# Expert weights in runs of 4 KB, three of four down blocks as fp32r passes, 128-column stationary operands

## The chip, the cores and the metric

The kernel runs on one core of one Trainium2 chip. The metric is the device time of one launch in microseconds. Three runs of the kernel before took 1442.43 to 1444.31 us, with a median of 1444.3 us. One further execution was profiled; all rows below are from it.

## The reference

One encoder layer on 1024 tokens of width 1024, in float32: a modulated RMSNorm, a combined input projection, latent attention and differential attention, an output projection, and a mixture of experts. Only the last part is touched by the change:

```python
# top-1 group of 4, then top-2 of 8 experts in it; 32 experts in all
g = xb @ w_gate[e]                     # xb: the rows routed to expert e, 1024 wide
u = xb @ w_up[e]                       # w_gate, w_up: 1024 x 512
ys = (jax.nn.silu(g) * u) @ w_down[e]  # w_down: 512 x 1024
out = out.at[row_token].add(ys * row_weight)
```

After it the residual is added and a last RMSNorm is applied. Each expert has 6 MB of weights, 201 MB for all 32.

## The kernel before

Everything ahead of the experts (projections, both attentions, output projection, router) takes the first 790 us or so and is left as it is, but for the weight loads that already start there. Then the 32 experts follow one another in a loop that is unrolled in Python (L1386). Each works on C = 96 rows, which a gather on POOL fetches from h2_d by index. The instructions stand in the order in which the code writes them; nothing reorders them, and each engine takes its own in that order.

**Precision.** A float32 product on TensorE is done in one of two ways. The first is a plain f32 matmul, which the profile shows as two instructions. The second is `mm3` (L66 to L69): both operands are split into a high part, rounded to fp32r, and a low part, the rest; three fp32r matmuls (high by high, high by low, low by high) add up in PSUM. A weight is split by `split_e` (L1149 to L1154): ScalarE casts 128x1024 values to the high part (L1152), VectorE subtracts to get the low part (L1153). Gate and up use `mm3`; down uses plain f32.

**Weights.** `load_w` (L1129) loads six pieces of 1 MB per expert: four of gate and up, with four row blocks of 128 x 512 each, in runs of 2 KB (a partition p holds rows p, 128 + p, 256 + p, 384 + p), and two of down, each all four row blocks of one half of the columns, again in runs of 2 KB. They go into 14 buffers. `load_free` (L1139) marks a piece as used and starts the next load: at first 14 pieces ahead, from the queue of SP; from piece 84 on the distance shrinks step by step to 7, and then the loads are issued from ScalarE's queue, between its computing instructions.

**Splits.** `split_to` (L1159) issues splits ahead of their use: a gate or up chunk (two of the eight row blocks, one split) asks for splits up to five chunks ahead (three from expert 28 on). The split parts live in a ring of 14 buffers (`ring_a`), two per split; one of the 14 holds `gate2` throughout, so at most six splits are alive.

**One expert e on TensorE:** 24 fp32r passes of gate (four chunks); 4 transposes of the hidden rows of expert e - 1 (`hidden_T`, L1338); 24 passes of up; down of expert e - 1 for the first 512 columns (`down`, L1344); 8 transposes of the rows of expert e + 1 (`x_T`, L1364); down for the other 512 columns; then POOL scatters the result, with accumulation, into x2_d. VectorE scales the down result per column half (L1351). After expert 20, `further_blocks` (L1287) is computed once on VectorE and POOL. The last expert's rows are not scattered but added by a matmul with a selection matrix (L1443), while x2_d is read back for the last norm; that read waits for the scatter of expert 30.

The stationary operand of all these matmuls is 128 x 96: one column for each of the 96 rows.

Of the kernel before, what the change touches and what calls it, by code (L numbers as in the profile page):

```python
# [46 lines left out]


@with_exitstack
def tile_hymba(  # L50
# [689 lines left out]
    wu = w_expert_up[0].rearrange("e (k p) f -> e p k f", p=128)  # L740
# [581 lines left out]
    def flip4(src, b):  # L1322
        ptr = ps4.tile([128, 512], F32, name="ptr4", tag="tr")[:, 0:4 * C]
        for i in range(4):
            j = 4 * b + i
            T.transpose(ptr[:, i * C:(i + 1) * C], src[:, j * 128:(j + 1) * 128], ident[:C, :C])  # L1326
        return ptr

    def glu_gate(pg):
        sg = mp.tile([C, DE], F32, name="sg", tag="sg", bufs=1)  # L1330
# [4 lines left out]
        V.tensor_mul(sg, sg, pu)  # L1335
        return sg

    def hidden_T(hm):  # L1338
        ptr = flip4(hm, 0)
        hT = mp.tile([128, 4, C], F32, name="hmT", tag="hmT")  # L1340
        V.tensor_copy(hT.rearrange("p a b -> p (a b)"), ptr)
        return hT

    def down(hT, w, y, n, wcol):  # L1344
        e, w = (w, raws["d", w, n]) if isinstance(w, int) else (None, w)

        pd = ps4.tile([128, 512], F32, name="pd", tag="pd")[:C]
        for k in range(4):
            T.matmul(pd, hT[:, k], w[:, k], start=k == 0, stop=k == 3)  # L1349
        ns = slice(n * 512, n * 512 + 512)  # L1350
        V.scalar_tensor_tensor(y[:, ns], pd, wcol, gate2[:, ns], op0=ALU.mult, op1=ALU.mult)  # L1351
        load_free(("d", e, n))

    def y_tile():
        return mp.tile([C, D], F32, name="y4", tag="y4")

    def half_ps(name, rows=C):
        return ps4.tile([128, DE], F32, name=name, tag=name)[:rows]
# [3 lines left out]
            gather(xbufs[e % NX], tg[:, e:e + 1])  # L1362

    def x_T(xb):  # L1364
        xT = mp.tile([128, 2, 8, C], F32R, name="xT", tag="xT")
        for b in range(2):
            ptr = flip4(xb, b)
            o = [xT[:, l, 4 * b:4 * b + 4].rearrange("p a b -> p (a b)") for l in range(2)]
            A.copy(o[0], ptr)  # L1369
            V.tensor_sub(o[1], ptr, f32(o[0]))  # L1370
        return xT

    def chunk(ps, xT, e, ch):
        split_to(8 * e + ch + 1 + (LEAD if e < ES else LEAD1))
        hi, lo = splits[8 * e + ch]
# [8 lines left out]
    x_in(NX)  # L1384
    prev = None
    for e in range(NE):  # L1386
        pg, pu = half_ps("pg"), half_ps("pu")
        for ch in range(4):
            chunk(pg, xT, e, ch)
        if prev:  # L1390
            hT, y = hidden_T(prev), y_tile()
        sg = glu_gate(pg)
        if e == 0:
            row(5 * D, gate2)
        for ch in range(4, 8):
            chunk(pu, xT, e, ch)
        hm = glu_up(sg, pu)
        if prev:
            down(hT, e - 1, y, 0, wt[:, e - 1:e])
            if e == NE - 1:  # L1400
                hT_last = hidden_T(hm)
# [26 lines left out]
    y = y_tile()  # L1428
    for n in range(2):
        down(hT_last, NE - 1, y, n, wt[:, NE - 1:])  # L1430
    yl = [mp.tile([C, D], F32R, name="yl", tag="xT") for _ in range(2)]
# [42 lines left out]
    with tc.For_i(0, nb, 1) as i:  # L1474
        er = Y.value_load(eii[0:1, 0, bass.ds(i, 1)], min_val=0, max_val=NE - 1)
        cr = mp.tile([128, NBM + 2], F32, name="cr", tag="cr")
        V.scalar_tensor_tensor(cr[:, 0:NBM], io, blk, ei[:, 1], op0=ALU.is_equal, op1=ALU.mult)
        V.reduce_sum(cr[:, NBM:NBM + 1], cr[:, 0:NBM], axis=AX.X)
        V.tensor_scalar(blk, blk, 1.0, None, op0=ALU.add)
        ats, tws = tile_a(F32)[:, 0:C], tile_a(F32)[:, 0:2 * NT].rearrange("p (t k) -> p t k", k=2)  # L1480
        ptw = ps4.tile([128, 512], F32, name="ptw", tag="tr")[:C]
        V.tensor_scalar(ats, iot_s, float(NE), cr[:, NBM:NBM + 1], op0=ALU.mult, op1=ALU.add)
        for j in range(2 * NT):
            t, k = divmod(j, 2)
            oa, tw = (mp.tile([128, w], F32, name=n, tag=n) for w, n in ((C, "oa"), (2, "tw")))
# [18 lines left out]
        hT = hidden_T(glu_up(glu_gate(pgu[0]), pgu[1]))
        y = y_tile()
        for n in range(2):
            down(hT, raw_w(wd[bass.ds(er, 1), :, :, n * 512:(n + 1) * 512].rearrange("a p k f -> (a p) k f")), y, n,
                 cr[:C, NBM + 1:NBM + 2])
# [45 lines left out]
```

## Time and profile before

| | |
|---|---|
| median of three runs | 1444.3 us |
| the profiled execution: own time, span | 1447.06 us, 1445.3 us |
| TensorE busy | 1337.1 us (93% of the span) |
| TensorE weight loads | 961.9 us (67%), beside the matmuls |
| VectorE busy | 993.9 us (69%) |
| ScalarE busy | 681.8 us (47%) |
| POOL busy | 416.9 us (29%) |
| DMA | 361.22 MB, 250 GB/s on average |
| mean granted TensorE clock | 0.962 |

The span is the time from the first to the last instruction; the profiled execution's own time is 1.8 us longer. Shares are averages over stages that have different limits, so the stretch of the experts, from about 790 to 1410 us, is to be read by itself.

### The profile page before, as it was taken

What the parts mean: (1) busy time and instruction counts of PE and PEld (TensorE: products, weight loads), DVE (VectorE), ACT (ScalarE), POOL (GpSimd) and SP (SyncE); (2) the same over time, 40 slices, a digit from 0 to 9 for tenths busy, and PEclk for the clock granted to TensorE, in tenths of its full rate; (3) what the DMA queues carried; (4) which work ended last, traced back from release to release, by engine and by line L of the source; (5) the groups of instructions that cost most, each with busy time, mean ns of one, the idle gap of its engine ahead of it and who ended that gap; (6) DMA issues with size and microseconds to landing.
All of it is one profiled execution on the core that took longest, in us unless ns stands there. A gap on an engine that the chain in (4) does not pass through costs nothing. (4 is left out here: it accounts for less than half of the span.)

```text
span 1445.3 us, 17733 instructions
## 1 busy us (share of the span) xinstructions
PE 1337.1 (93%) x6211; PEld 961.9 (67%) x6211; DVE 993.9 (69%) x1530; ACT 681.8 (47%) x1058; POOL 416.9 (29%) x285
## 2 busy tenths in 40 slices
PE   5799896998999999989995999999999998999993
PEld 4578676986788888878884655566565555656541
DVE  6888553475788888884568766676766668666646
ACT  4642212454766666661214554444554444544523
POOL 3100000002766666650002233333333322111231
PEclk9899898999999999999995999999999999999995
DMA  9537799268043433337968999999988998999956
GB/s 328 150 100 249 198 298 209 55 223 302 1 152 125 139 130 140 132 112 261 340 224 297 339 354 315 348 366 354 345 297 297 327 348 308 347 359 338 372 181 238
DMA packets 197502, 361.22 MB, mean 250 GB/s; under 512 B 20101, under 2 KB 62146, under 8 KB 195874
## 3 DMA queue, kind: packets, MB, share of 16 engines
q1 hardware_dynamic: 132946, 228.97, 47.2%
q10 hardware_dynamic: 57024, 113.25, 21.9%
q0 software_dynamic: 7440, 17.84, 5.2%
q8 instruction: 50, 0.82, 0.2%
q14 instruction: 42, 0.34, 0.1%
HBM read 306.52 MB, written 61.88 MB: 255 GB/s over the span
## 5 line engine op out<-in xcount | busy, mean ns | idle before, releaser
L1153 DVE TENSOR_TENSOR ra<-rb,ra 128x1024 fp32r<-128x1024 f32 x180 | 210.8, 1217 | 42.4 <-ACT ra L1152 42.2
L1152 ACT CAST ra<-rb 128x1024 fp32r<-128x1024 f32 x180 | 181.5, 1050 | 93.4 <-PE pg L69 34.2
L1319 POOL DMA_INDIRECT x_d<-y,tg x32 | 139.2, 4351 | 132.5 <-DVE y L1351 130.3
L1349 PE MATMUL pd<-rb,hmT 128*96 128x512 f32 x368 | 165.1, 592 | 0.0
L604 PE MATMUL s<-ra 128*128 128x512 f32 x448 | 129.5, 405 | 2.5 <-ACT e L625 2.4
L1351 DVE SCALAR_TENSOR_TENSOR y<-pd,wt,ra 96x512 f32<-96x512 f32 x64 | 47.8, 747 | 121.5 <-PE pd L1349 121.5
L67 PE MATMUL pz<-whi,hThi 128*128 128x512 f32 (+2 forms) x320 | 122.3, 382 | 9.6 <-ACT hThi L255 5.1
L625 ACT ACTIVATE e<-s,mx 128x1024 f32<-128x1024 f32 x96 | 107.6, 1120 | 38.5 <-DVE mx L620 21.8
L620 DVE TENSOR_REDUCE mx<-s 128x1 f32<-128x1024 f32 x96 | 116.6, 1217 | 12.2 <-PE s L604 12.2
L68 PE MATMUL pz<-wlo,hThi 128*128 128x512 f32 (+2 forms) x320 | 120.6, 377 | 1.5 <-DVE wlo L131 1.5
L930 POOL DMA_INDIRECT xb<-h_d,tg x31 | 31.5, 1017 | 313.4 <-PE ptr L1326 312.8
L69 PE MATMUL pz<-whi,hTlo 128*128 128x512 f32 (+2 forms) x320 | 116.0, 370 | 0.3 <-DVE hTlo L257 0.3
L67 PE MATMUL pg<-ra,xT 128*96 128x512 f32 x256 | 114.1, 446 | 0.2 <-ACT xT L1369 0.2
L1349 PEld LDWEIGHTS pd<-rb,hmT 128*96 128x96 f32 x368 | 58.2, 163 | 77.6 <-issue 74.5
L68 PE MATMUL pu<-ra,xT 128*96 128x512 f32 x256 | 102.6, 401 | 3.7 <-DVE ra L1153 3.7
L69 PE MATMUL pg<-ra,xT 128*96 128x512 f32 x256 | 102.1, 399 | 2.8 <-DVE xT L1370 2.8
L67 PE MATMUL pu<-ra,xT 128*96 128x512 f32 x256 | 103.7, 405 | 0.0
L1153 DVE TENSOR_TENSOR ra<-rx,ra 128x1024 fp32r<-128x1024 f32 x76 | 89.6, 1217 | 19.2 <-ACT ra L1152 19.2
L636 ACT CAST rb<-ptr 128x512 fp32r<-128x512 f32 x128 | 74.4, 588 | 59.8 <-PE ptr L632 59.2
L68 PE MATMUL pg<-ra,xT 128*96 128x512 f32 x256 | 102.0, 398 | 0.0
L69 PE MATMUL pu<-ra,xT 128*96 128x512 f32 x256 | 100.7, 393 | 0.0
L1152 ACT CAST ra<-rx 128x1024 fp32r<-128x1024 f32 x76 | 76.8, 1047 | 38.6 <-PE pg L69 11.5
(336 smaller groups left out, 2813.2 us busy)
## 6 DMA issues: line engine op xcount, KB each, us to landing
rb<-in_w_expert_up_dram ACTq DMA_DIRECT2D x26, 1024.0 KB, 16.7
rb<-in_w_expert_down_dram ACTq DMA_DIRECT2D x26, 1024.0 KB, 9.2
rb<-in_w_expert_gate_dram ACTq DMA_DIRECT2D x24, 1024.0 KB, 12.7
rb<-in_w_expert_gate_dram SPq DMA_DIRECT2D x20, 1024.0 KB, 15.6
rb<-in_w_expert_down_dram SPq DMA_DIRECT2D x20, 1024.0 KB, 9.2
rb<-in_w_expert_up_dram SPq DMA_DIRECT2D x19, 1024.0 KB, 10.3
aw<-in_w_ada_dram SPq DMA_DIRECT2D x32, 512.0 KB, 5.0
ra<-qk_d SPq DMA_DIRECT2D x24, 512.0 KB, 6.0
```

Of the source, the lines that this page charges most:

```text
L67: T.matmul(ps, ahi, bhi, start=first, stop=False)
L68: T.matmul(ps, ahi, blo, start=False, stop=False)
L69: T.matmul(ps, alo, bhi, start=False, stop=last)
L604: T.matmul(ps[:, ns], l, r[:, ns], start=i == 0, stop=i == len(parts) - 1)
L620: V.reduce_max(mx, ps, axis=AX.X, negate=True)
L625: A.activation(e, ps, AF.Exp, bias=nb, scale=1.0, accum_out=z)
L636: A.copy(hi[:, :, q], src)
L1152: A.copy(hi, raw[:, 2 * half:2 * half + 2])
L1153: V.tensor_sub(lo, raw[:, 2 * half:2 * half + 2], f32(hi))
L1319: G.indirect_dma_start(out=x2_d, out_offset=bass.IndirectOffsetOnAxis(ap=si, axis=0), in_=y, in_offset=None, bounds_check=S - 1, oob_is_er ...
L1349: T.matmul(pd, hT[:, k], w[:, k], start=k == 0, stop=k == 3)
L1351: V.scalar_tensor_tensor(y[:, ns], pd, wcol, gate2[:, ns], op0=ALU.mult, op1=ALU.mult)
```

## The change

Three edits, all in the expert stage. First, row blocks are formed differently: a gate or up piece holds, per partition, two times two neighbouring rows (4 KB runs), and x's columns are picked with a step of two to match (`x_cols`); a down piece holds two whole row blocks of 1024 columns (4 KB runs). Second, three of the four row blocks of down are split and done with `mm3` (DS = 3), one stays plain f32; the splits of down stand in one list (`todo`) with those of gate and up, and the hidden rows are split as well; down now goes over the row blocks, with both column halves in two PSUM tiles, and the two scaling instructions come at its end (`put_y`). Third, each stationary operand is read 128 columns wide (`wide`): 32 columns of the next block, or of a zeroed pad, come along, and the rows of PSUM that they make are not read. The x operands (`xTs`) and the hidden operands (`hs4`) become fixed buffers.

```diff
+DS = 3
-    wg = w_expert_gate[0].rearrange("e (k p) f -> e p k f", p=128)
+    wg = w_expert_gate[0].rearrange("e (q p j) f -> e p q (j f)", p=128, j=2)
-            eng.dma_start(r, (wg, wu)[i // 2][e, :, 4 * (i % 2):4 * (i % 2) + 4] if kind == "g" else
-                          wd[e, :, :, 512 * i:512 * i + 512])
+            eng.dma_start(r.rearrange("p (q j) f -> p q (j f)", j=2),
+                          ((wg, wu)[i // 2] if kind == "g" else wd)[e, :, 2 * (i % 2):2 * (i % 2) + 2])
+    todo = [("g", 0, ch) for ch in range(8)]
+    for e in range(1, NE):
+        todo += [("g", e, ch) for ch in range(8)] + [("d", e - 1, ch) for ch in range(DS)]
+    todo += [("d", NE - 1, ch) for ch in range(DS)]
...
+    def x_cols(xb, b):
+        v = xb.rearrange("c (q p j) -> c q j p", p=128, j=2)
+        return [v[:, 2 * b + i // 2, i % 2] for i in range(4)]
+    def wide(t, i):
+        return t[:, i * C:i * C + 128]
...
-        hT = mp.tile([128, 4, C], F32, name="hmT", tag="hmT")
-        V.tensor_copy(hT.rearrange("p a b -> p (a b)"), ptr)
+        A.copy(hT[:, 0:DS * C], ptr[:, 0:DS * C])
+        V.tensor_sub(hT[:, DS * C:2 * DS * C], ptr[:, 0:DS * C], f32(hT[:, 0:DS * C]))
+        if DS < 4:
+            A.copy(hF[:, 0:(4 - DS) * C], ptr[:, DS * C:])
...
-        for k in range(4):
-            T.matmul(pd, hT[:, k], w[:, k], start=k == 0, stop=k == 3)
+        for k in (2 * half, 2 * half + 1):
+            if k < DS:
+                split_to(at_of["d", e, k] + 1 + LEAD1)
+                hi, lo = splits[at_of["d", e, k]]
+                hi, lo = (w.rearrange("p a f -> p (a f)") for w in (hi, lo))
+                for n in range(2):
+                    ns = slice(n * 512, n * 512 + 512)
+                    mm3(pds[n], wide(hT, k), wide(hT, DS + k), hi[:, ns], lo[:, ns], k == 0, k == 3)
+            else:
+                w = raws["d", e, half].rearrange("p (k j) f -> p k (j f)", j=2)[:, k % 2]
+                for n in range(2):
+                    T.matmul(pds[n], wide(hF, k - DS), w[:, n * 512:n * 512 + 512], start=k == 0, stop=k == 3)
+        if 2 * half + 1 >= DS:
+            load_free(("d", e, half))
...
-            mm3(ps, xT[:, 0, k], xT[:, 1, k], hi[:, k2], lo[:, k2], k == 0, k == 7)
+            mm3(ps, wide(xT, k), wide(xT, 8 + k), hi[:, k2], lo[:, k2], k == 0, k == 7)
...
         if prev:
-            down(hT, e - 1, y, 1, wt[:, e - 1:e])
+            down(hT, e - 1, 1, pds)
+            put_y(pds, y, wt[:, e - 1:e])
             scatter(y, tg[:, e - 1:e])
```

## Rows read from the trace of the kernel before

**Rows 1.** Busy time by stretch: us, then engines, clock, DMA share, GB/s.
```profile
800.00:1400.00 600.00, 594.48 (x2372) 353.31 (x2371) 404.49 (x455) 289.51 (x342) 171.16 (x65) 1.00 0.97 333
888.00:926.00 38.00, 38.00 (x154) 22.54 (x153) 25.67 (x28) 18.48 (x22) 13.02 (x5) 1.00 1.05 369
1192.00:1230.00 38.00, 34.31 (x131) 19.68 (x130) 29.30 (x37) 16.69 (x20) 7.57 (x3) 0.96 0.89 307
```

**Rows 2.** Timeline of TensorE over one expert: start us, us, instruction, count.
```profile
1002.10 0.45 PE L67 MATMUL pu<-ra,xT 128*96 128x512 f32 x1
...
1007.77 3.60 PE L1349 MATMUL pd<-rb,hmT 128*96 128x512 f32 x8
1011.20 0.83 PE L1326 MATMUL ptr<-ident,xb 96*128 96x96 f32 x8
1011.86 3.60 PE L1349 MATMUL pd<-rb,hmT 128*96 128x512 f32 x8
...
1020.87 0.49 PE L1326 MATMUL ptr<-ident,sg 96*128 96x96 f32 x4
1021.14 0.45 PE L67 MATMUL pu<-ra,xT 128*96 128x512 f32 x1
```

**Rows 3.** Timeline of TensorE, 128-column stationary operands: output projection, input projection.
```profile
737.12 0.39 PE L67 MATMUL pm<-rb,vt 128*128 128x512 f32 x1
...
745.06 0.39 PE L69 MATMUL pm<-rb,vt 128*128 128x512 f32 x1
...
109.65 0.39 PE L69 MATMUL pz<-whi,hTlo 128*128 128x512 f32 x1
...
111.73 0.40 PE L69 MATMUL pz<-whi,hTlo 128*128 128x512 f32 x1
```

**Rows 4.** Groups by line and shape, 740 to 1400 us: weight loads (busy us, mean ns).
```profile
L68 PEld LDWEIGHTS pg<-ra,xT 128*96 128x96 f32 x256 | 42.0, 164 | 24.1 <-issue 8.0
...
L68 PEld LDWEIGHTS pm<-rb,vt 128*128 128x128 f32 x25 | 4.7, 188 | 0.9
```

**Rows 5.** Timeline of VectorE and ScalarE over one expert (idle before, releaser in brackets).
```profile
1002.36 0.56 DVE L1341 COPY hmT<-ptr 128x384 f32<-128x384 f32 x1 [0.61 <-PE ptr L1326]
1002.85 3.88 ACT L1152 CAST ra<-rx 128x1024 fp32r<-128x1024 f32 x4
...
1015.50 0.75 DVE L1351 SCALAR_TENSOR_TENSOR y<-pd,wt,ra 96x512 f32<-96x512 f32 x1 [2.23 <-PE pd L1349]
...
1022.97 4.63 DVE L1153 TENSOR_TENSOR ra<-rb,ra 128x1024 fp32r<-128x1024 f32 x4 [1.01 <-ACT ra L1152]
```

**Rows 6.** DMA queues, 800 to 1400 us: packets, MB, share; then a stretch's busy row.
```profile
q10 hardware_dynamic: 57024, 113.25, 52.7%
q1 hardware_dynamic: 35571, 71.05, 33.1%
q0 software_dynamic: 6608, 15.37, 10.8%
...
623.00:627.00 4.00, 3.79 (x19) 2.91 (x20) 4.00 (x7) 3.57 (x8) 1.96 (x3) 1.00 0.98 388
```

**Rows 7.** Timeline of ScalarE's queue: loads that it issues, late in the experts.
```profile
1265.25 0.52 ACTq L1136 DMA_DIRECT2D rx<-in_w_expert_gate_dram  x1
...
1266.38 3.96 ACTq L1136 DMA_DIRECT2D rx<-in_w_expert_up_dram  x1
...
1270.54 5.01 ACTq L1136 DMA_DIRECT2D rb<-in_w_expert_down_dram  x1
```

**Rows 8.** Timeline of VectorE after expert 20.
```profile
1189.58 0.49 DVE L1292 TENSOR_TENSOR ra<-cnt,thr 128x320 f32<-128x320 f32 x1 [1.98 <-POOL thr L1289]
...
1196.78 3.49 DVE L1153 TENSOR_TENSOR ra<-rx,ra 128x1024 fp32r<-128x1024 f32 x3
```

**Rows 9.** Timeline at the end of the experts.
```profile
1401.21 0.75 DVE L1351 SCALAR_TENSOR_TENSOR y<-pd,wt,ra 96x512 f32<-96x512 f32 x1 [2.56 <-PE pd L1349]
1402.24 1.51 POOL L1319 DMA_INDIRECT x_d<-y,tg  x1 [8.06 <-DVE y L1351]
...
1407.86 4.71 SPq L1426 DMA_DIRECT2D rb<-x_d  x8
```

More of the change, by code (lines that the diff above doesn't have):

```diff
@@ L1157, in tile_hymba @@
     splits = []
+    todo = [("g", 0, ch) for ch in range(8)]
+    for e in range(1, NE):
+        todo += [("g", e, ch) for ch in range(8)] + [("d", e - 1, ch) for ch in range(DS)]
+    todo += [("d", NE - 1, ch) for ch in range(DS)]
+    at_of = {c: i for i, c in enumerate(todo)}
     def split_to(n):
-        while len(splits) < min(n, 8 * NE):
-            e, ch = divmod(len(splits), 8)
-            key = "g", e, ch // 2
+        while len(splits) < min(n, len(todo)):
+            kind, e, ch = todo[len(splits)]
+            key = kind, e, ch // 2
             if key not in raws:
@@ L1314, in raw_w @@
         r = tile_b(F32, 4, 512)
-        Y.dma_start(r, src)
+        Y.dma_start(r.rearrange("p (q j) f -> p q (j f)", j=2), src)
         return r
@@ L1320, in scatter, with flip4, stat @@
                              in_=y, in_offset=None, bounds_check=S - 1, oob_is_err=False, compute_op=ALU.add)
-    def flip4(src, b):
+    def flip4(cols):
         ptr = ps4.tile([128, 512], F32, name="ptr4", tag="tr")[:, 0:4 * C]
         for i in range(4):
-            j = 4 * b + i
-            T.transpose(ptr[:, i * C:(i + 1) * C], src[:, j * 128:(j + 1) * 128], ident[:C, :C])
-        return ptr
+            T.transpose(ptr[:, i * C:(i + 1) * C], cols[i], ident[:C, :C])
+        return ptr
+    def x_cols(xb, b):
[3 more added lines that the diff above has]
+        return t[:, i * C:i * C + 128]
+    def stat(pool, name, n, dtype=F32R):
+        t = pool.tile([128, n * C + 128 - C], dtype, name=name) if pool else tile_a(dtype)[:, :n * C + 128 - C]
+        G.memset(f32(t[:, n * C:]), 0.0)
+        return t
     def glu_gate(pg):
@@ L1336, in glu_up, with h_cols, hidden_T, down @@
         return sg
-    def hidden_T(hm):
-        ptr = flip4(hm, 0)
-        hT = mp.tile([128, 4, C], F32, name="hmT", tag="hmT")
-        V.tensor_copy(hT.rearrange("p a b -> p (a b)"), ptr)
[L1342 to L1347, printed above, removed]
-        for k in range(4):
-            T.matmul(pd, hT[:, k], w[:, k], start=k == 0, stop=k == 3)
-        ns = slice(n * 512, n * 512 + 512)
-        V.scalar_tensor_tensor(y[:, ns], pd, wcol, gate2[:, ns], op0=ALU.mult, op1=ALU.mult)
-        load_free(("d", e, n))
+    def h_cols(hm):
+        return [hm[:, i * 128:(i + 1) * 128] for i in range(4)]
+    def hidden_T(hm, hT, hF):
+        ptr = flip4(h_cols(hm))
+        A.copy(hT[:, 0:DS * C], ptr[:, 0:DS * C])
+        V.tensor_sub(hT[:, DS * C:2 * DS * C], ptr[:, 0:DS * C], f32(hT[:, 0:DS * C]))
+        if DS < 4:
+            A.copy(hF[:, 0:(4 - DS) * C], ptr[:, DS * C:])
+        return hT, hF
+    def down(h, e, half, pds):
+        hT, hF = h
+        for k in (2 * half, 2 * half + 1):
[12 more added lines that the diff above has]
+            load_free(("d", e, half))
+    def pd_tiles():
+        return [ps4.tile([128, 512], F32, name="pd", tag="pd") for _ in range(2)]
+    def put_y(pds, y, wcol):
+        for n in range(2):
+            ns = slice(n * 512, n * 512 + 512)
+            V.scalar_tensor_tensor(y[:, ns], pds[n][:C], wcol, gate2[:, ns], op0=ALU.mult, op1=ALU.mult)
     def y_tile():
@@ L1364, in x_T @@
     def x_T(xb):
-        xT = mp.tile([128, 2, 8, C], F32R, name="xT", tag="xT")
+        xTs.reverse()
+        xT = xTs[0]
         for b in range(2):
-            ptr = flip4(xb, b)
-            o = [xT[:, l, 4 * b:4 * b + 4].rearrange("p a b -> p (a b)") for l in range(2)]
+            ptr = flip4(x_cols(xb, b))
+            o = [xT[:, (8 * l + 4 * b) * C:(8 * l + 4 * b + 4) * C] for l in range(2)]
             A.copy(o[0], ptr)
@@ L1373, in chunk @@
     def chunk(ps, xT, e, ch):
-        split_to(8 * e + ch + 1 + (LEAD if e < ES else LEAD1))
-        hi, lo = splits[8 * e + ch]
+        at = at_of["g", e, ch]
+        split_to(at + 1 + (LEAD if e < ES else LEAD1))
+        hi, lo = splits[at]
         for k2 in range(2):
             k = 2 * (ch % 4) + k2
-            mm3(ps, xT[:, 0, k], xT[:, 1, k], hi[:, k2], lo[:, k2], k == 0, k == 7)
+            mm3(ps, wide(xT, k), wide(xT, 8 + k), hi[:, k2], lo[:, k2], k == 0, k == 7)
+    xTs = [stat(xp, "xT%d" % i, 16) for i in range(2)]
+    hs4 = stat(xp, "hT", 2 * DS), stat(xp, "hF", 4 - DS, F32)
     for i in range(1, NX):
@@ L1386, in tile_hymba @@
     for e in range(NE):
[L1387 removed]
+        pg, pu = half_ps("pg", 128), half_ps("pu", 128)
         for ch in range(4):
@@ L1390, in tile_hymba @@
         if prev:
-            hT, y = hidden_T(prev), y_tile()
-        sg = glu_gate(pg)
+            hT, y, pds = hidden_T(prev, *hs4), y_tile(), pd_tiles()
+        sg = glu_gate(pg[:C])
         if e == 0:
@@ L1396, in tile_hymba @@
             chunk(pu, xT, e, ch)
-        hm = glu_up(sg, pu)
+        hm = glu_up(sg, pu[:C])
         if prev:
-            down(hT, e - 1, y, 0, wt[:, e - 1:e])
+            down(hT, e - 1, 0, pds)
             if e == NE - 1:
-                hT_last = hidden_T(hm)
+                hT_last = hidden_T(hm, stat(None, "", 2 * DS), stat(None, "", 4 - DS, F32))
         if e < NE - 1:
@@ L1427, in tile_hymba @@
     A.activation(st[:, 0, 3:4], epsc, AF.Sqrt)
[L1428 to L1431, printed above, removed]
+    y, pds = y_tile(), pd_tiles()
+    for half in range(2):
+        down(hT_last, NE - 1, half, pds)
+    put_y(pds, y, wt[:, NE - 1:])
+    yl = [t[:C, 0:D] for t in xTs]
     for n in range(2):
@@ L1500, in tile_hymba @@
             for j in range(2):
-                raw = raw_w(w[bass.ds(er, 1), :, 4 * j:4 * j + 4].rearrange("a p k f -> (a p) k f"))
+                raw = raw_w(w[bass.ds(er, 1), :, 2 * j:2 * j + 2].rearrange("a p k f -> (a p) k f"))
                 for k in range(4):
                     T.matmul(pgu[g], xT[:, 4 * j + k], raw[:, k], start=j + k == 0, stop=j + k == 4)
[L1504 to L1508, printed above, removed]
+        ptr = flip4(h_cols(glu_up(glu_gate(pgu[0]), pgu[1])))
+        hF = tile_a(F32)[:, 0:4 * C]
+        V.tensor_copy(hF, ptr)
+        y, pds = y_tile(), pd_tiles()
+        for j in range(2):
+            raw = raw_w(wd[bass.ds(er, 1), :, 2 * j:2 * j + 2].rearrange("a p k f -> (a p) k f"))
+            raw = raw.rearrange("p (k j) f -> p k (j f)", j=2)
+            for k in range(2):
+                for n in range(2):
+                    T.matmul(pds[n][:C], hF[:, (2 * j + k) * C:(2 * j + k + 1) * C], raw[:, k, n * 512:n * 512 + 512],
+                             start=j + k == 0, stop=j + k == 2)
+        put_y(pds, y, cr[:C, NBM + 1:NBM + 2])
         scatter(y, iv)
```

4 lines of the change are left out of this document (2 added, 2 removed).

## The prediction

> **What bounds the kernel now.** I read the busy time by stretch first. Over 800 to 1400 us, which holds the experts, TensorE is busy 594.5 of 600 us at full clock, VectorE 404, ScalarE 290, and the DMA engines show a share of 0.97 [rows 1]. So TensorE sets the pace, and the DMA engines are nearly full beside it. The timeline of TensorE shows how an expert is made up [rows 2]: from one start of up to the next it is 1021.14 - 1002.10 = 19.04 us. Up (24 passes) takes 1007.77 - 1002.10 = 5.67. One half of down, 8 instructions, takes 1011.20 - 1007.77 = 3.43 (0.429 each); the other half the same. The 8 transposes of x take 0.66. Gate runs from 1011.86 + 3.43 = 1015.29 to 1020.87, 5.58 us; the 4 transposes of the hidden rows take 0.27. These add up to 19.04, so there is no idle in it, and what shortens TensorE's instructions shortens the kernel until another engine or the DMA stops it. A pass with a 96-column stationary operand costs 5.58/24 to 5.67/24 = 0.233 to 0.236 us.
>
> **The change part by part.**
>
> Down on TensorE. Before: 16 instructions of 0.429 = 6.86 us. After: one f32 row block, 2 column halves of 2 instructions, 4 x 0.429 = 1.72 us, and 3 row blocks x 2 halves x 3 passes = 18 fp32r passes. How long is a pass with 128 columns? The output projection has 35 intervals from 737.12 to 745.06, 0.227 us each; the input projection 9 from 109.65 to 111.73, 0.231 [rows 3]. The weight load itself gets longer, 188 ns in place of 164 [rows 4], but it lies under the pass before it (0.227 or more), so I charge nothing for it; if it ever stood alone it would cost 24 ns x 66 passes = 1.6 us an expert. I take 0.231, the middle of what the rows give: 18 x 0.231 = 4.16, down 5.88, a saving of 0.98 us. Gate and up have 48 passes; at 0.231 in place of 0.233 (the better of the two 96-column values) they give 0.10. Together 1.08 us an expert, 19.04 to 17.96. Ends: at 0.227, 6.86 - 5.81 + 48 x 0.006 = 1.34; at 0.236 for all 128-column passes, 6.86 - 5.97 - 48 x 0.003 = 0.75. Down of experts 0 to 30 stands ahead of the end that counts (below): 31 x 1.08 = **-33.5 us** (-23 to -42).
>
> VectorE. Two experts keep it busy 25.67 us [rows 1], 12.8 each. Added: three subtractions of 128x1024. Four in a row take 4.63 us, so one takes 1.14 more [rows 5]: +3.4. The copy of 0.56 us [rows 5] becomes a subtraction on three quarters of the columns, 0.45. The sum is 16.1 us in 17.96, 90%. It fits only if its order lets it. I walked through it with t = 0 at the end of down. The two scalings come first now, 0.2 to 1.7; then the subtractions for chunks 3, 4, 5 of gate and up end at 2.8, 4.0, 5.1; TensorE wants them at 4.2, 5.9, 7.3. Chunks 6 and 7 end at 6.3 and 7.5 (wanted 8.7, 10.1), the three down blocks and the hidden rows between 8.6 and 11.4 (wanted from 11.5 on), the next expert's chunks 0 and 1 at 12.5 and 13.7, glu at 14.4, the x parts by 16.2 after their transposes, chunk 2 at 17.4, before the next scalings at 18.2. The smallest margin is 1.4 us. So it costs nothing as long as nothing holds VectorE up by more than that.
>
> ScalarE. Per expert 9.24 us now [rows 1], plus three casts at 0.97 (3.88 for four [rows 5]) = 2.9, plus about 0.6 for the hidden rows by their share of columns: 12.8. To this come six DMA issues of about 0.5 when nothing blocks them [rows 7], 3.0: 15.8 of 17.96. It fits, and runs ahead of VectorE except where the ring is full. Cover gone, its price is the second rival.
>
> 4 KB runs. Queue q10 moved 113.25 MB in 52.7% of 600 us = 316 us of all engines, 358 GB/s, in runs of 2 KB [rows 6]. An expert's 6.29 MB then take 17.6 us, and the gathers and scatters (q0, 10.8% of 600 us over 31.5 experts) 2.1: 19.7 us for a period of 19.04. The DMA is now behind by 0.6 us an expert, and the reserve of 14 loads pays for it. Loads of w_out in runs of 4 KB ran at 388 GB/s with a share of 0.98 [rows 6], 396 when full: 15.9 + 2.1 = 18.0 us, the new period. With the reserve on top it is no bound; at 358 it would be one (first rival). By itself this edit gives nothing, but without it the rest would not come through.
>
> A step of two in x's columns. The transposes of x load 128 columns of x as the stationary operand, now with a step of two elements. The trace has no such load. The 8 transposes take 0.66 us [rows 2]; the ends are no cost and twice that, +0.66 us an expert or +20 us. I take zero, as the loads lie beside the 96-column streams. [...]
>
> further_blocks. After expert 20 VectorE is held from 1187.6 to 1196.78 by it [rows 8] (2.0 of it a wait for POOL), and TensorE idles 38 - 34.31 = 3.7 us in that stretch [rows 1]. In the new order the scalings end at t = 1.7, so chunk 3 is subtracted by 1.7 + 9.2 + 1.1 = 12.0, when TensorE wants it at 4.2: 7.8 us of idle, **+4 us** against now (0 to +8).
>
> The end. The read of x2_d (1407.86) waits for the scatter of expert 30, which was issued at 1402.24 after the second scaling, 1401.21 [rows 9]. Both scalings now stand between the end of down and that scatter: **+0.7 us**. The last expert's own down lies beside this wait, so its saving is not counted, and its longer way (both scalings, then the casts) has some 5 us of cover there. The four small memsets on POOL are about a microsecond, 18 us ahead of need: nothing.
>
> The sum: -33.5 + 4 + 0.7 = -28.8. From the profiled execution's 1447.06 this is 1418.3; that execution is 2.8 above the median of the runs, so **1415.5, I say 1415 us**.
>
> **The rivals.**
>
> The DMA sets the pace. For it: a share of 0.97 to 1.05 [rows 1], and a need of 18.0 us in a period of 17.96 even at the better rate. If 4 KB runs go no faster than 2 KB ones, the 184.3 MB of q10 and q1 in this stretch take 515 us at 358 GB/s plus 65 for q0, 580 us from 800 on, as now; TensorE then waits for weights and the time stays at 1440 to 1445 us, say 1442. Against it: the w_out loads above. [...]
>
> ScalarE is held by its DMA issues: slower. Late in the experts single issues take 3.96 and 5.01 us [rows 7], when several megabytes are outstanding; ScalarE does not compute past them once its queue is empty. Now it has the room, with 9.2 of 19 us. With 12.8 us of work, four issues at 0.5 and two blocked ones of 9.0 in sum it needs 23.8 us; at three quarters of that blocking, 6.75 us, 21.6. Over the 20 experts from 1012 us on, whose loads ScalarE issues, that is 20 x 3.6 = 72, less 29: +43, 1487 us. It decides from a blocking of 4.6 us an expert on (12.8 + 2 + 4.6 = 19.4, where 20 x 1.45 eats the 29). Against it: runs of 4 KB halve the descriptors, the eight loads of x2_d (4 MB in 4 KB runs) are issued in 4.71 us, 0.59 each [rows 9], and the pieces come free more evenly, as the first down piece is free after its split.
>
> The saving is half eaten. Either the step of two doubles the transposes (1415 + 20 = 1435), or VectorE, at 90%, is held up some 0.6 us an expert by its waits for PSUM, of which there is one of 2.23 us now [rows 5]: the period becomes 18.6 and the time 1435. For it: the thin margin of 1.4 us. Against it: VectorE waits there now because it has nothing left to do.
>
> That 128 columns do nothing for a pass is inside the first forecast: the 0.236 end, 1426.
>
> **How the numbers follow.** The forecast, 1403 to 1430 us: 0.66. Half eaten, 1430 to 1440: 0.12. DMA bound, 1440 to 1445: 0.08. ScalarE blocked, above 1450: 0.10. Faster than 1403, if small idle of now (5.5 us in 600) goes too: 0.04. What can be told from no change is 0.2%, 3 us. Faster: 0.66 + 0.12 + 0.04 and 0.03 of the DMA case, 0.85; same 0.04; slower 0.11. The range 1402 to 1438 leaves out some 0.18.
>
> **What would show it.** Right: a period of 17.8 to 18.1 us between two starts of up, down in 5.9 us, VectorE near 90%, a load rate near 390 GB/s, single issues on ScalarE's queue near 0.5 us, an idle of some 8 us on TensorE after expert 20. Wrong: TensorE waiting for VectorE's L1153 counterpart in each expert, casts that wait for weight loads, passes well off 0.231, or transposes of x well above 0.66 us.

## The result and the profile after

The kernel after takes 1427.5 us (median of four runs, 1425.5 to 1429.1), beside 1443.8 us for the kernel before in the same series (1442.4 to 1444.3). The ratio is 0.9888, with a 95% interval of 0.9871 to 0.9905: some 16 us faster. I had said 1415 us. The profiled execution took 1428.1 us with a span of 1426.4 us, 18.9 us shorter than the span before.

Busy time by stretch (us; then TensorE, its weight loads, VectorE, ScalarE, POOL; clock, DMA share, GB/s), to be held against [rows 1]:

```profile
800.00:1400.00 600.00, 587.62 (x2589) 457.15 (x2589) 510.77 (x564) 394.85 (x509) 255.66 (x69) 0.99 0.94 340
888.00:926.00 38.00, 38.00 (x172) 29.90 (x171) 33.21 (x37) 25.00 (x32) 17.63 (x4) 1.00 1.02 372
```

TensorE still has no idle time in a regular stretch of two experts (38.00 of 38 us). VectorE went from 25.67 to 33.21 of 38 us, ScalarE from 18.48 to 25.00.

The timeline of TensorE over one expert, as in [rows 2] but from one start of gate to the next:

```profile
1002.87 0.80 PE L68 MATMUL pg<-ra,xT 128*128 128x512 f32 x1
...
1008.87 0.49 PE L1333 MATMUL ptr<-ident,sg 96*128 96x96 f32 x4
1009.14 0.48 PE L68 MATMUL pu<-ra,xT 128*128 128x512 f32 x1
...
1014.81 0.40 PE L68 MATMUL pd<-ra,hT 128*128 128x512 f32 x1
...
1017.60 1.08 PE L1333 MATMUL ptr<-ident,xb 96*128 96x96 f32 x8
1018.47 0.48 PE L68 MATMUL pd<-ra,hT 128*128 128x512 f32 x1
...
1019.94 1.88 PE L1386 MATMUL pd<-rb,hF 128*128 128x512 f32 x4
1021.26 0.80 PE L68 MATMUL pg<-ra,xT 128*128 128x512 f32 x1
```

The period is 18.39 us here, 18.38 over most experts, in place of 19.04. Up takes 1014.81 - 1009.14 = 5.67 us, exactly what it took with 96 columns. Down's 18 passes take 2.79 + 1.47 = 4.26. The 8 transposes of x take 1018.47 - 1017.60 = 0.87, where they took 0.66.

The DMA queues between 800 and 1400 us, as in [rows 6]; 29376 packets in place of 57024 for the same bytes, and 113.25 MB in 49.4% of 600 us is 382 GB/s:

```profile
q10 hardware_dynamic: 29376, 113.25, 49.4%
...
q0 software_dynamic: 6720, 15.71, 11.2%
```

Loads issued from ScalarE's queue, late in the experts (against [rows 7]); of all 108 from this queue one takes 1.56 us, the others under 0.9, where 28 took over 1 us before:

```profile
1266.72 0.37 ACTq L1138 DMA_DIRECT2D rb<-in_w_expert_gate_dram  x1
1267.12 0.49 ACTq L1138 DMA_DIRECT2D rb<-in_w_expert_gate_dram  x1
1267.67 0.46 ACTq L1138 DMA_DIRECT2D rb<-in_w_expert_up_dram  x1
1268.27 0.85 ACTq L1138 DMA_DIRECT2D rb<-in_w_expert_up_dram  x1
```

VectorE after expert 20 (against [rows 8]): the scalings end, then `further_blocks` holds it until 1178.93.

```profile
1168.36 1.40 DVE L1397 SCALAR_TENSOR_TENSOR y<-pd,wt,ra 96x512 f32<-96x512 f32 x2
1171.74 0.49 DVE L1300 TENSOR_TENSOR ra<-cnt,thr 128x320 f32<-128x320 f32 x1 [1.98 <-POOL thr L1297]
...
1178.93 1.21 DVE L1155 TENSOR_TENSOR ra<-rb,ra 128x1024 fp32r<-128x1024 f32 x1
```

What TensorE waited for in that stretch (us in total, times, longest), first the kernel before, then the kernel after:

```profile
PE pu L68 <- DVE ra L1153: 3.7, 1, 3.7
```

```profile
PE pg L69 <- DVE ra L1155: 6.9, 1, 6.9
```

The wait is not all that it costs. Behind the idle the passes start 0.43 us apart and not 0.235, and the granted clock from 1178 to 1184 us is 0.50:

```profile
1172.88 0.39 PE L68 MATMUL pg<-ra,xT 128*128 128x512 f32 x1
1180.20 0.79 PE L69 MATMUL pg<-ra,xT 128*128 128x512 f32 x1 [6.93 <-DVE ra L1155]
1180.79 0.63 PE L70 MATMUL pg<-ra,xT 128*128 128x512 f32 x1
1181.22 0.63 PE L68 MATMUL pg<-ra,xT 128*128 128x512 f32 x1
```

From 1172.88 to the first pass at full pace again (1184.37) there are nine passes and four transposes, 2.4 us of work at the usual pace, in 11.49 us: 9.1 us are lost. Before, eight passes took 7.13 us (1193.97 to 1201.10): 5.2 lost.

The end of the experts (against [rows 9]):

```profile
1379.52 1.02 PE L1386 MATMUL pd<-rb,hF 128*128 128x512 f32 x2
1380.69 1.22 DVE L1155 TENSOR_TENSOR ra<-rb,ra 128x1024 fp32r<-128x1024 f32 x1 [1.25 <-ACT ra L1154]
1381.83 1.40 DVE L1397 SCALAR_TENSOR_TENSOR y<-pd,wt,ra 96x512 f32<-96x512 f32 x2
...
1383.51 1.50 POOL L1327 DMA_INDIRECT x_d<-y,tg  x1 [9.78 <-DVE y L1397]
...
1389.18 2.80 SPq L1476 DMA_DIRECT2D rb<-x_d  x6
```

From the first scaling to the read of x2_d it is now 7.35 us; before, from the one scaling that stood there, 6.65: the difference is the 0.7 of the second scaling. But the first scaling starts 1.3 us behind the last f32 matmul, not at once, because VectorE first subtracts the last expert's third down block (1380.69).

### The profile page after: what moved, and what is told of

Same layout as the page of the kernel before. It is cut to its first block, busy times and chain, and to the rows that moved or that the text cites. A ratio compares the mean times of both kernels' runs of the same rounds, so it can differ in the third digit from the quotient of the medians.

```text
span 1426.4 us, 18460 instructions
## 1 busy us (share of the span) xinstructions
PE 1317.7 (92%) x6403; PEld 1062.5 (74%) x6403; DVE 1094.6 (77%) x1626; ACT 783.8 (55%) x1218; POOL 499.1 (35%) x291
## 3 DMA queue, kind: packets, MB, share of 16 engines
q10 hardware_dynamic: 29376, 113.25, 20.8%
## 5 line engine op out<-in xcount | busy, mean ns | idle before, releaser
L1155 DVE TENSOR_TENSOR ra<-rb,ra 128x1024 fp32r<-128x1024 f32 x249 | 290.4, 1219 | 51.6 <-ACT ra L1154 46.6
L1327 POOL DMA_INDIRECT x_d<-y,tg x32 | 222.8, 6963 | 123.2 <-DVE y L1397 108.2
L1154 ACT CAST ra<-rb 128x1024 fp32r<-128x1024 f32 x249 | 242.4, 1048 | 1.9 <-PE pg L69 1.3
L1155 DVE TENSOR_TENSOR ra<-rx,ra 128x1024 fp32r<-128x1024 f32 x103 | 120.5, 1216 | 16.9 <-ACT ra L1154 15.0
L68 PE MATMUL pg<-ra,xT 128*128 128x512 f32 x256 | 114.9, 449 | 0.1
L69 PE MATMUL pg<-ra,xT 128*128 128x512 f32 x256 | 102.5, 401 | 6.9 <-DVE ra L1155 6.9
L68 PE MATMUL pu<-ra,xT 128*128 128x512 f32 x256 | 104.1, 407 | 0.0
L70 PE MATMUL pg<-ra,xT 128*128 128x512 f32 x256 | 103.0, 402 | 1.1 <-DVE xT L1416 1.1
L1154 ACT CAST ra<-rx 128x1024 fp32r<-128x1024 f32 x103 | 101.2, 1048 | 2.3 <-DMA rb<-in_w_expert_down_dram 1.4
L70 PE MATMUL pu<-ra,xT 128*128 128x512 f32 x256 | 101.3, 396 | 0.0
L69 PE MATMUL pu<-ra,xT 128*128 128x512 f32 x256 | 101.2, 395 | 0.1
L835 POOL TENSOR_SCALAR e<-e,zd 128x1024 f32<-128x1024 f32 x32 | 36.0, 1124 | 172.2 <-DVE zd L834 172.2
L605 PEld LDWEIGHTS s<-ra 128*128 128x128 f32 x448 | 81.1, 190 | 19.8 <-ACT e L626 4.3
L638 DVE TENSOR_TENSOR rb<-ptr,rb 128x512 fp32r<-128x512 f32 x128 | 86.3, 679 | 10.2 <-ACT rb L637 10.1
```

The lines of the kernel that those rows point to most:

```text
L68: T.matmul(ps, ahi, bhi, start=first, stop=False)
L69: T.matmul(ps, ahi, blo, start=False, stop=False)
L70: T.matmul(ps, alo, bhi, start=False, stop=last)
L605: T.matmul(ps[:, ns], l, r[:, ns], start=i == 0, stop=i == len(parts) - 1)
L638: return lambda: V.tensor_sub(lo[:, :, q], src, f32(hi[:, :, q]))
L835: G.tensor_scalar(e1, e1, zd[:, 2:3], 1.0, op0=ALU.mult, op1=ALU.mult)
```

## The experiments

**How to compare them.** Each kernel was timed beside the kernel before on its chip; the ratio to it is what counts. One more thing is needed to read the profiles. The last matmul of the input projection, a stage that no kernel here changes, starts anywhere between 292.3 and 301.7 us, and all that follows shifts with it (before: 295.7, after: 292.3, so 3.4 of the 18.9 us by which the two spans differ come from there). I therefore also give "the rest": from the first matmul of the output projection to the end of the span, in which this shift is not contained. The period is the distance between two multiplications of glu on VectorE (sg<-sg,pu).

| kernel | ratio to before (95%) | period, us | the rest, us |
|---|---|---|---|
| before | 1 | 19.04 | 793.4 |
| after | 0.9888 (0.9871 to 0.9905) | 18.38 | 778.1 |
| after, second chip | 0.9888 (0.9866 to 0.9909) | 18.38 | 776.6 |
| 96 columns | 0.9871 (0.9852 to 0.9890) | 18.27 | 775.6 |
| x columns neighbouring | 0.9852 (0.9833 to 0.9872) | 18.12 | 769.9 |
| the same with 2 KB runs | 1.0050 (1.0034 to 1.0067) | 18.12 and stalls | 798.4 |
| further_blocks in pieces | 0.9836 (0.9816 to 0.9856) | 18.38 | 770.7 |
| DS = 4, 96 columns | 0.9841 (0.9817 to 0.9865) | 18.00 | 771.3 |
| DS = 2 | 0.9953 (0.9935 to 0.9971) | 18.69 | 785.0 |
| all together, DS = 3 | 0.9824 (0.9800 to 0.9848) | 18.03 | 766.3 |
| better placed, DS = 3 | 0.9809 (0.9780 to 0.9838) | 18.03 | 763.5 |
| better placed, DS = 4 | 0.9772 (0.9742 to 0.9801) | 17.74 | 758.2 |
| 4 KB runs alone, DS = 0 | 0.9996 (0.9976 to 1.0016) | 19.02 | 792.9 |

My theory after the result: the gain is only the f32 instructions that became fp32r passes; it fell short because the width gives nothing and because the step of two in x lengthens the transposes; `further_blocks` costs its 7 us; the 4 KB runs keep the loads from binding. The rivals: the width matters, the length of the runs doesn't, VectorE already binds.

**Stationary operands of 96 columns.**

```diff
-        return t[:, i * C:i * C + 128]
+        return t[:, i * C:i * C + C]
...
```

> The kernel after with the stationary operands read 96 columns wide again, as before the change; all else as after (1427.5 us). Theory (all of the gain is that three of four row blocks of down take 18 fp32r passes in place of f32, the width does nothing): passes stay at 0.232 to 0.236 us, weight loads fall from 188 to 164 ns beside them, period 18.39 us as after, time 1426 to 1429 us. Rival (the width gives what the prediction took, 0.003 to 0.006 us a pass on 66 passes an expert): period 0.2 to 0.4 us longer, time 1434 to 1440 us.

Weight loads of gate, 740 to 1400 us (busy us, mean ns | idle before), first the kernel after, then 96 columns:

```profile
L68 PEld LDWEIGHTS pg<-ra,xT 128*128 128x128 f32 x256 | 49.0, 191 | 17.5 <-ACT ra L1154 7.2 <-ACT xT L1415 0.5
```

```profile
L68 PEld LDWEIGHTS pg<-ra,xT 128*96 128x96 f32 x256 | 42.0, 164 | 24.6 <-ACT ra L1154 8.0 <-ACT xT L1415 0.5
```

Two periods of the 96-column kernel: (982.04 - 945.51)/2 = 18.27 us.

```profile
945.51 0.68 DVE L1357 TENSOR_TENSOR sg<-sg,pu 96x512 f32<-96x512 f32 x1
963.74 0.68 DVE L1357 TENSOR_TENSOR sg<-sg,pu 96x512 f32<-96x512 f32 x1
982.04 0.68 DVE L1357 TENSOR_TENSOR sg<-sg,pu 96x512 f32<-96x512 f32 x1
```

The period gets shorter with 96 columns, by 0.11 us, 1.7 ns for each of 66 passes. The rival has the wrong sign. In time, 0.9871 against 0.9888 is not told apart. With the other two edits in place, the 128 columns give nothing.

**x's columns neighbouring.**

```diff
-        v = xb.rearrange("c (q p j) -> c q j p", p=128, j=2)
-        return [v[:, 2 * b + i // 2, i % 2] for i in range(4)]
+        return [xb[:, (4 * b + i) * 128:(4 * b + i + 1) * 128] for i in range(4)]
```

> The kernel after, but x's columns are picked as 128 neighbouring ones, no longer with a step of two. The weights stay in runs of 4 KB, so that gate and up multiply each column of x with another row's weights: the amounts of work are the same, the sums of gate and up are not the reference's. Theory (the step of two makes the 8 transposes of x longer, 0.87 us in place of 0.66): they fall back to 0.66 us, period 18.18 us, 31 x 0.21 = 6.5 us gained, time 1420 to 1423 us. Rival (the transposes are longer for another reason, such as the order of the work around them or DMA writes into x's buffers): 0.87 us and 1426 to 1429 us as after.

The stationary loads of the x transposes, 800 to 1390 us, first the kernel after, then this one:

```profile
L1333 PEld LDWEIGHTS ptr<-ident,xb 96*128 96x128 f32 x245 | 34.1, 213 | 2.6
```

```profile
L1333 PEld LDWEIGHTS ptr<-ident,xb 96*128 96x128 f32 x248 | 24.0, 140 | 4.3
```

A load takes 213 ns with the step and 140 without; the period falls by 0.26 us (expected 0.21), the rest by some 7.5 us, the ratio by 0.0036 (the two intervals just touch). The step is the cause, the rival is out.

**The same with runs of 2 KB.** Gate and up as in the kernel before; a down piece in two loads:

```diff
-            eng.dma_start(r.rearrange("p (q j) f -> p q (j f)", j=2),
-                          ((wg, wu)[i // 2] if kind == "g" else wd)[e, :, 2 * (i % 2):2 * (i % 2) + 2])
+            if kind == "g":
+                eng.dma_start(r, (wg, wu)[i // 2][e, :, 4 * (i % 2):4 * (i % 2) + 4])
+            else:
+                for n in range(2):
+                    eng.dma_start(r[:, 2 * n:2 * n + 2], wd[e, :, 2 * i:2 * i + 2, n * 512:n * 512 + 512])
...
```

> The kernel after, but all expert weights are loaded in runs of 2 KB (gate and up in the row blocks of before; a down piece as two loads of one column half each, so two more issues an expert), and x's columns are neighbouring ones, as these row blocks need. To be compared with the same change to x's columns alone. Theory (at 2 KB the queue moves some 358 GB/s, 17.6 us an expert, and with gathers and scatters 19.7 us are needed in a period of 18.2: the loads bind once the reserve of 14 pieces is used up): TensorE waits for weights late in the experts, q10 near 358 GB/s with a DMA share near 1, time 1435 to 1443 us. Rival (the run's length does not set the rate, or the reserve and the smaller load of the tail carry it): no waits for loads, 1420 to 1424 us, as with the x columns alone.

It is slower than the kernel before. Against the kernel above, which differs by the runs (and two more issues an expert), it loses 28 us of the rest. Busy time ahead of the stall and in it, the queue from 800 to 1390 us, and two casts on ScalarE with what they waited for:

```profile
960.00:980.00 20.00, 20.00 (x91) 15.59 (x91) 17.89 (x20) 12.89 (x17) 8.83 (x2) 1.00 1.04 341
...
1012.00:1018.00 6.00, 0.00 (x0) 0.00 (x0) 0.00 (x0) 0.00 (x0) 0.00 (x0) 0.67 1.04 393
1018.00:1024.00 6.00, 3.68 (x8) 2.59 (x9) 2.36 (x2) 1.99 (x2) 0.00 (x0) 0.50 1.05 393
```

```profile
q10 hardware_dynamic: 57621, 113.24, 54.0%
```

```profile
1018.76 1.04 ACT L1158 CAST ra<-rx 128x1024 fp32r<-128x1024 f32 x1 [13.28 <-DMA rb<-in_w_expert_up_dram]
...
1027.59 1.04 ACT L1158 CAST ra<-rb 128x1024 fp32r<-128x1024 f32 x1 [6.84 <-DMA rb<-in_w_expert_down_dram]
```

For nine periods it takes 18.1 us an expert; then one period takes 38.15 us. In the middle of it no engine computes while the DMA engines are full (share 1.04). TensorE itself waits 9.03 and 3.61 us in it and three times under 0.5; behind these waits its passes are 0.43 us apart, at a granted clock of 0.50. Over the stage the queue moved 113.24 MB in 54.0% of 590 us, 355 GB/s. That is what the runs of 2 KB reach beside the experts' work and not the most that they can: in the stall they move 393 GB/s. The theory had it right that the loads bind, and put the price too low (1435 to 1443 us, which is 0.994 to 0.9995 of before; measured 1.005). Where it went wrong: I spread the deficit over the experts, and it comes in one stall, in which casts wait 13.28 and 6.84 us for loads. Why all at once is not shown: the cast at 1018.76 reads a tile of up whose load SP had issued some 30 us earlier (two loads of up into rx, from 982.24 on), with the DMA engines full all the time (shares of 0.99 to 1.05); and the stall stands where the loads go over from SP's queue to ScalarE's, whose first issue is at 1003.00.

**The 4 KB runs alone.** The edit of the x columns, 96 columns, and `DS = 0`; the new order of down stays.

> The runs of 4 KB alone: the kernel after with no row block of down split (DS = 0, all four as plain f32), 96 columns, and x's columns neighbouring, so that gate and up multiply each column of x with another row's weights (amounts of work as in the reference, sums not). Theory (loads did not bind in the kernel before, its reserve carried them, so longer runs give nothing by themselves): period 19.04 us as before, 0.997 to 1.003 of before. Rival (part of the gain comes from the loads: the periods of 19.2 to 24.5 us of the kernel before in its last third were waits for weights): these go, 5 us or more less than before, ratio 0.996 or less.

Ratio 0.9996. The queue (800 to 1390 us) runs at 113.25 MB in 50.6% of 590 us, 379 GB/s, and nothing comes of it:

```profile
q10 hardware_dynamic: 29376, 113.25, 50.6%
```

TensorE waits once in the regular experts, as long as in the kernel before:

```profile
PE pu L69 <- DVE ra L1155: 3.7, 1, 3.7
```

ScalarE's casts wait for loads 4 times between 800 and 1400 us, and 21 times in the kernel before; TensorE waits for none of them. With the run before this settles the part of the runs: nothing by themselves, 28 us where the period is 18.12.

**further_blocks in pieces.** Cut into six parts, one behind each of experts 16 to 21:

```diff
-        if e == 20:
-            further_blocks()
+        if 16 <= e < 22:
+            further_blocks(e - 16)
...
```

> The kernel after, but further_blocks is issued in six pieces, one behind each of experts 16 to 21, of which none holds VectorE longer than 2 us (the two large steps in two halves); the result is the same. Theory (the 6.9 us that TensorE idles after expert 20 are VectorE's 9.2 us, POOL's 2.0 among them, in front of the splits): the idle falls to under 1 us, 6 to 7 us gained, time 1420 to 1423 us. Rival (the idle is made good elsewhere, since the loads run ahead in the meantime, or each piece costs part of it since VectorE is at 87% anyway): 1424 to 1428 us.

TensorE's wait on a split in this stretch falls from 6.9 to 1.3 us:

```profile
PE pg L69 <- DVE ra L1155: 1.3, 2, 0.9
```

The ratio falls by 0.0052 (7.5 us), the rest by some 6.7 us, more than the 5.6 us of idle: the granted clock stays at 1.00 in this stretch (1178 to 1216 us, 0.92 in the kernel after). The idle was real and was VectorE's.

**Two and four blocks split.** The edit of the first is shown; the second has `DS = 4`, 96 columns and no pads.

```diff
-DS = 3
+DS = 2
```

> Two of four row blocks of down split (DS = 2), else the kernel after. Theory (each block that goes from f32 to split passes saves 8 x 0.43 / 2 - 6 x 0.232 = 0.33 us an expert, and the period is TensorE's alone): period 18.71 us, 10 us slower than after, ratio to before 0.996. Rival (VectorE or the loads already cost something at DS = 3, and the third block bought less than the second): period below 18.6 us, less than 6 us slower than after, ratio 0.992 or less.

> All four row blocks of down split (DS = 4, no f32 passes left), with stationary operands 96 columns wide and without the pads, which do not fit beside the fourth block's parts; to be compared with the 96-column run with DS = 3, whose period was 18.27 us. Theory (TensorE's passes alone set the period): 24 passes in place of 18 and 4 x 0.43 us: 18.27 - 1.72 + 6 x 0.232 = 17.94 us, 31 x 0.33 = 10 us less, ratio to before 0.980. Rival (VectorE binds: 16.1 us of work an expert become 17.4 us, and its order no longer fits; or the loads, which took 366 GB/s of some 375, bind): periods stay at 18.2 us or more, TensorE waits for VectorE's subtractions or for loads in most experts, ratio 0.986 or more.

Expert periods, DS = 2 (969.32 - 950.62 = 18.70) and DS = 4 (966.11 - 948.11 = 18.00):

```profile
950.62 0.68 DVE L1357 TENSOR_TENSOR sg<-sg,pu 96x512 f32<-96x512 f32 x1
969.32 0.68 DVE L1357 TENSOR_TENSOR sg<-sg,pu 96x512 f32<-96x512 f32 x1
```

```profile
948.11 0.68 DVE L1356 TENSOR_TENSOR sg<-sg,pu 96x512 f32<-96x512 f32 x1
966.11 0.68 DVE L1356 TENSOR_TENSOR sg<-sg,pu 96x512 f32<-96x512 f32 x1
```

The third block buys 18.69 - 18.38 = 0.31 us an expert (0.33 expected), the fourth, between the two 96-column kernels, 0.27. In time DS = 2 loses 0.0065 of before, 9 us, as expected. DS = 4 gains 0.0030 (4 us) against 96 columns with DS = 3 and not 10; the two intervals overlap. In its profile VectorE is at 36.24 of 38 us in a stretch of two experts, and the rest is 4.3 us shorter, where 31 x 0.27 would be 8.4. TensorE's waits for a split in gate, first with 96 columns and DS = 3, then with DS = 4:

```profile
PE pg L69 <- DVE ra L1155: 7.0, 1, 7.0
```

```profile
PE pg L69 <- DVE ra L1155: 8.8, 2, 8.4
```

The wait behind `further_blocks` is 1.5 us longer, and the one in the last expert's down 1.6 us longer (1.92 at 1373.42, against 0.29), which is most of the difference. One period is 20.27 us, of which the next two give back all but 0.6; there a cast waits 2.80 us for a load (1017.87). That the two longer waits come from VectorE's missing slack fits, but no run here tried it. VectorE does not bind at DS = 3.

**Put together.** 96 columns, `further_blocks` in pieces, the split of the last expert's third down block held back, and h2 stored so that x's columns are neighbouring with the 4 KB runs:

```diff
-            V.scalar_tensor_tensor(h2s[t][:, ns], x2s[t][:, ns], st[:, 6:7], G2[:, ns], op0=ALU.mult, op1=ALU.mult)
-            V.tensor_add(h2s[t][:, ns], h2s[t][:, ns], B2[:, ns])
+            o = h2s[t][:, ns].rearrange("c (j m) -> c j m", j=2)
+            xi, gi, bi = (a[:, ns].rearrange("c (m j) -> c j m", j=2) for a in (x2s[t], G2, B2))
+            V.scalar_tensor_tensor(o, xi, st[:, 6:7], gi, op0=ALU.mult, op1=ALU.mult)
+            V.tensor_add(o, o, bi)
...
```

> The runs so far put together, the reference's result: 96-column stationary operands; further_blocks in six pieces; h2 stored with even columns ahead of odd ones in each half (the router's weight rows in the same order), so that x's columns for the 4 KB runs are neighbouring; the split of the last expert's third down block held back behind the scaling of expert 30. DS = 3. Theory (the parts add up): 3.4 for the width, 7 for x's columns, 6.6 for further_blocks, 1.2 for the tail, 18 us less than after: ratio to before 0.975 to 0.978, periods of 18.0 us. Rival (a faster TensorE meets the loads, which already took 366 of some 375 GB/s, or the norm's strided reads on VectorE ahead of the experts cost 4 us or more): TensorE waits for loads late in the experts, ratio 0.980 or more.

Periods of 18.03 us, as the parts say, but 0.9824 and not 0.975 to 0.978: 766.3 of rest is 10.3 less than after on that chip, not 18. Four periods with a piece in them are 18.96, 18.89, 19.75 and 19.75, so the pieces cost some 5 us, of which the next five give back 1.6. The last period is 20.79, 1 us longer than after, and the held-back split gave nothing. Ahead of the first glu the way from the first matmul of the output projection is 154.4 us, 2.8 more than after; this is where the norm reads x2 with a step. The two kernels below have the same norm and take 152.8 and 151.8, so that it costs 2.8 us is not shown. The theory's sum fails, and the rival's loads are not the reason: none of TensorE's waits between 740 and 1425 us is for one.

**Better placed, DS = 3 and 4.** Parts 3 to 5 of `further_blocks` go behind the last down, where VectorE waited 3.53 us for that down and 2.43 us for x2_d in the run of all together:

```diff
...
+        if e in (16, 17, 19):
+            further_blocks((16, 17, 19).index(e))
...
+    for part in (3, 4, 5):
+        further_blocks(part)
```

> The combined kernel again (DS = 3, 96 columns, h2 stored so that x's columns are neighbouring, the reference's result), with further_blocks placed anew: its POOL part behind expert 16, its two small steps behind experts 17 and 19, and its two large steps and the end (4.8 us) at the very end of the experts, where VectorE waits 3.5 us for the last down and 2.4 us for x2_d; the POOL part of the last expert's selection matrix one expert earlier; the held-back split of the tail as in the kernel after. Theory (steps of VectorE cost TensorE what they exceed a slack of some 2 us an expert, and nothing where it waits): the 5 us that the pieces still cost in the combined run fall to 1, ratio to before 0.978 to 0.981 in place of 0.982. Rival (the tail is given away in return, since the last norm waits for VectorE): 0.982 to 0.984.

> The same with all four row blocks of down split (DS = 4). Theory (TensorE's passes set the period as long as VectorE's 17.3 us and the loads fit): period 18.03 - 0.27 = 17.76 us, 8 us less than with DS = 3, ratio 0.973 to 0.976. Rival (an expert's transfers, some 6.7 MB at the 366 to 379 GB/s seen so far, take 17.7 to 18.3 us, so the reserve of loads is used up and TensorE waits late in the experts; or VectorE at 97% has no slack left): no gain over DS = 3, 0.978 or more.

With DS = 3 the ratio is 0.9809, at the edge of what was expected, and its interval does not part it from 0.9824. With DS = 4 it is 0.9772: 33 us faster than the kernel before, and the fastest here. The period is 17.74 as forecast; the gain over DS = 3 is 5.3 us, not 8. ScalarE in that kernel, late in the experts:

```profile
1253.86 1.05 ACT L1159 CAST ra<-rb 128x1024 fp32r<-128x1024 f32 x1 [1.94 <-DMA rb<-in_w_expert_down_dram]
...
1267.82 1.05 ACT L1159 CAST ra<-rb 128x1024 fp32r<-128x1024 f32 x1 [1.37 <-DMA rb<-in_w_expert_up_dram]
1271.79 1.05 ACT L1159 CAST ra<-rb 128x1024 fp32r<-128x1024 f32 x1 [1.98 <-DMA rb<-in_w_expert_up_dram]
```

There the casts wait for loads, in a stretch (1240 to 1280 us) with a DMA share of 1.00, and two periods take 20.08 and 19.27 us, but the next takes 14.73. What counts is TensorE, which over all experts waits for splits in gate like this:

```profile
PE pg L69 <- DVE ra L1160: 2.9, 7, 0.6
```

Five of the seven waits, 2.1 us in all, lie between 1270 and 1327 us, where such casts stand. So the loads' rival shows, but costs TensorE some 2 us there at most. It is not tied to the period of 17.74 nor to the late experts alone: a cast waits 2.31 us for a load at 1009.00, in a period of 19.52 us, and with DS = 3, at 18.03, casts wait for loads from 1243.62 us on, up to 2.18 us. Where the rest of the missing gain went is not shown.

## Why the prediction was right or wrong

The direction was right, and the time lies in the range; the 1415 us were 12.5 too low. Nearly all of that is the period: 18.38 in place of 17.96, 31 x 0.42 = 13 us.

- **Down on TensorE.** Right in kind: DS = 2, 3 and 4 give 0.31 and 0.27 us a block, by TensorE's instructions alone. The size was off. I took 0.231 us for a pass with 128 columns, from rows of other stages [rows 3]. Gate and the f32 block take 7.32 us together (from 1019.94 on, over the end of the period), up 5.67, the passes of down 4.26; less the f32 block's 1.72 that is 15.53 us for 66 passes, 0.235. The gain of 0.10 on gate and up was none, and down's passes took 0.10 more. That 128 columns do nothing stood in the text as the end of 0.236, with 1426 us. The better price was that of the same passes in the same place, 0.233 to 0.236 [rows 2].
- **The step of two.** This is the step that failed in kind: taken at zero, within ends of 0 and +0.66 us an expert. It is 0.21 by the timeline, 0.26 by the experiment, 7 us in all. I reasoned that the loads lie beside the streams of 96 columns. But without the step the eight loads already keep the loader busy 24.0/31 = 0.77 us an expert, and the transposes take 0.66 from start to end: by these figures nothing was left under which a longer load could hide, and with the step it is 34.1/31 = 1.1 us. A load with the step takes 213 ns, without it 140.
- **VectorE.** Right: 33.21/38 x 18.38 = 16.1 us an expert, as summed, and no wait of TensorE for it in the regular experts. With DS = 4 it is at 95%, and half of what TensorE saved was lost, most of it in two longer waits for splits.
- **ScalarE.** 12.1 us where I had 12.8; issues of 0.37 to 0.85 us, but for one of 1.56. The rival of blocked issues did not come. It begins to show at shorter periods: in the two better placed kernels 13 (DS = 3) and 30 (DS = 4) of 108 issues take over 1 us, up to 4.2 and 4.7 us. How ScalarE fares beside a long issue, the trace of before shows: behind the start of the one of 3.96 us (1266.38) the next cast starts at 1270.44, 0.10 us after its end; in the one of 5.01 us (1270.54) a cast starts at 1271.40 and none more until 1275.67, 0.12 us after its end.
- **The runs.** Both halves of the sentence hold: nothing by themselves (0.9996), and without them the rest does not come through (1.005). The rate was 382 GB/s, not the 396 that I worked out from the loads of w_out, so an expert needs 16.5 us and 2.1 for gathers and scatters, 18.6 in a period of 18.38: by this estimate the loads just fit, with the reserve. Had the period been the 17.96 that I forecast, 0.6 us an expert would have been missing. The first rival's 358 GB/s are not what binds here: runs of 4 KB gave 382, and runs of 2 KB 355 beside the experts' work and 393 in the stall.
- **further_blocks.** 7.8 us of idle forecast, 6.9 measured, against 3.7 before. With the slow passes behind the idle, which I left out on both sides, it is 9.1 against 5.2, so +3.9 where I had +4. Right in kind; that the number meets is in part luck, as 0.9 less idle and 0.7 more of slow passes nearly cancel.
- **The end.** The 0.7 us are there, and 1.1 more: I had listed the splits of down for the last expert, but not that one of them stands ahead of the scalings on VectorE. That is read from the timeline alone: with that split held back, in the run of all together, the end got no shorter. The memsets of the pads take 0.12 to 0.14 us each (770 to 790 us).

Part by part, 31 x 0.66 = -20.5, +3.9 and +1.8 make -14.8 us; the rest went from 793.4 to 778.1 and 776.6, and the medians differ by 16.3. What the last 0.5 to 2 us are is open.

## What to carry to other kernels

Take the price of an instruction from the same instruction beside the same neighbours; a slightly better figure from another stage is not a gain until something shows what makes it better. When an operand's layout changes, ask whether its load is already longer than what hides it (here 0.77 us of loads beside 0.66 us of transposes). An edit that gives nothing alone may carry another one: when the bounding engine gets faster, work out the next limit's need for the new period, and remember that a deficit need not show at once: with runs of 2 KB nine periods took 18.1 us, and the next 38.15. Look for slow passes behind an idle of TensorE and add them to it: here 2.2 us behind 6.9.

## What was not expected of the hardware

A float32 stationary load of 96x128 with a step of two took 213 ns, against 140 with neighbouring columns. POOL's scatter into x2_d got longer: with DS = 0, then in the kernel after (830 to 1170 us; busy us, mean ns):

```profile
L1327 POOL DMA_INDIRECT x_d<-y,tg x18 | 90.1, 5007 | 58.6 <-DVE y L1397 58.6
```

```profile
L1327 POOL DMA_INDIRECT x_d<-y,tg x18 | 141.2, 7843 | 55.2 <-DVE y L1397 55.2
```

5.0 us became 7.8 (5.5 in the kernel before), with the same rows and bytes. Between 888 and 926 us VectorE is busy 24.5 of 38 us with DS = 0 and 33.2 in the kernel after; whether that is the reason no run here tried, so the cause of the longer scatter stays open. The scatter lay off the path, except at the end of the experts. Last, the input projection, equal in all kernels, ended up to 9.4 us apart from profile to profile; why stays open, and it is as large as most of the effects studied here.
